# Gate projections between the attention's units, output by token tiles, one gate tile on another queue

## The chip, the cores and the metric

One core of one Trainium2 chip. The metric is device time in microseconds (us) of one execution. Three runs of the kernel before took 2414.84, 2416.75 and 2404.22 us; the median is 2414.84.

## The reference, cut to what matters

Two transformer layers run one after the other on x of 512 tokens by 1024 features, all in fp32. The first has a gated delta rule with four heads (`o_g`, chunks of 64 tokens, a state carried from chunk to chunk) and an attention with four heads (`o_n`: compressed, selected and windowed keys), then a gated feed-forward. The output of the delta rule is gated by a projection of the layer's input:

```python
o_g = rmsnorm(o_g, gdn_out_norm_w) * jax.nn.silu(gz.reshape(hd))
mixed = jnp.concatenate([o_g, o_n], axis=-1)
x = x + gate1 * (mixed @ w_out)
```

The second layer ends in a mixture of 16,384 experts: each token takes 16 of them for each of 8 heads, and the result is normalised.

```python
act = gelu(einsum('chkd,cd->chk', expert_u[experts], hc))
x = x + gate2 * einsum('chk,chkd->cd', gate * act, expert_v[experts])
return rmsnorm_2(x, final_g)
```

## The kernel before, in words

x is kept transposed: features on the 128 partitions in 8 blocks, 512 tokens along the row. A projection with 128 outputs is `gemm` (line 222): `weight` (line 200) loads 128x1024 fp32 through SP's queue, casts it on ScalarE (ACT) to a high part and subtracts on VectorE (DVE) for a low part (`split`, lines 196 to 198), and 8 blocks of three matmuls (high x high, high x low, low x high) fill one PSUM bank. The raw weight takes a buffer of the tag "raw" (three of them), the pair one of two.

The order of the instructions on each engine is not written by hand: a scheduler at build time takes them by the order of the code and by its own time model, and from then on each engine runs its queue in order. Buffers carry tags; a tile of a tag waits until one of that tag's buffers is free.

The first layer, from line 533: `nsa_begin`; for the pairs of heads (0, 1) and (2, 3) the projections q and v with `gdn_fin`, and `gdn_scan`, eight steps one after another that carry the state through small fp32 matmuls; then for the four tiles of 128 tokens, h = 0 to 3, the gate projection `proj_gz(h)` (line 661, its copy at line 662) and the attention `nsa(kp, h, h > 1)` (line 911). `nsa` has a compressed part (lines 921 to 941) and then four units, one per head (lines 942 to 968): two products of queries and keys, maximum, exponent into a tile "pr" of 128 x 2 x 512 (line 953), scaling, transposes through PSUM (line 963), copy to "pt", product with the values, copy of the result. "pr" has two buffers. Tiles 2 and 3 of the attention put the products into the two PSUM banks "acc", which the gate projections use too. At the end `gdn_out` (line 831) gates the scan's output, and the output projection follows.

The second layer's experts, `peer` (line 1127): a first stage forms the activations of all 128 groups of 128 experts, `spread` (line 1460) writes the gates of the tokens to DRAM in 22 blocks (a 23rd stays on the chip). The last stage, lines 1210 to 1280, goes through the 128 groups e: `gates` (line 1221) loads a gate tile for two groups (e = 0) or eight, from 22 blocks x 128 partitions, into "gtile" (two buffers); the activation is multiplied by its gate (line 1245), split, the group's 512 KB of weights are loaded and split, and `expert_out` adds into eight PSUM banks. Meanwhile `gather` (line 1323) fetches single experts' rows by indirect DMA on GpSimd's queue (POOL), and `gather_sum` (line 1336) adds them on DVE, 144 in all: 128 into `pN`, 16 into `pX`. After the last group the sums are folded into the banks (lines 1272 and 1273), x is updated, and `final` (line 1284) normalises: sums of squares over the features on TensorE, `r` by a power on GpSimd (line 1295), scaling by the gain (lines 1299 and 1301), transposes (line 1304), scaling by r (lines 1310 and 1312) and output (line 1313), one block of 128 features with all 512 tokens at a time.

Of the kernel before, what the change touches and what calls it, by code (L numbers as in the profile page):

```python
# [9 lines left out]
F32 = mybir.dt.float32  # L10
# [4 lines left out]
AF = mybir.ActivationFunctionType  # L15
ALU = mybir.AluOpType
# [4 lines left out]
P = 128  # L21
S = 512
D = 1024
KD = D // P
TT = S // P
# [129 lines left out]
class Builder:  # L155
# [304 lines left out]
    def block1(self):  # L460
        A, V, x = self.A, self.V, self.x
        with ExitStack() as st1:
            mp = self.mp = self.actp = self.pool(st1, "mp")
            gp = self.gp = self.pool(st1, "gd")
            self.ns = self.pool(st1, "ns")
            hst = ExitStack()
            hp = self.pool(hst, "h1", side="right")
            hi = hp.tile([P, KD, S], F32R, name="hi")
            lo = hp.tile([P, KD, S], F32R, name="lo")
            with ExitStack() as st2:  # L470
                self.ap = self.pool(st2, "ada", side="right")
                self.sqp = (self.ap, 3)
                for k in range(KD):
                    self.stat_add(k)
                self.dma(self.cols, A["cols"])
                self.sqp = (self.sm, 2)
                sw = self.cp.tile([P, KD], F32, name="swn1")
                ac = self.cp.tile([P, KD], F32, name="ac")
                self.C.activation(ac, self.col("c", 0, KD), AF.Silu)
                small = self.proj_small(hi, lo)  # L480
                started, weights = [], {}


                def mods(k):
                    v = self.mod(0, 1)[:, k:k + 1]
                    if k < 5:
                        self.dma(spare[k], A["ads"][k].rearrange("p k n -> p (k n)"))
                        ps = self.ps(5)
                        for i in range(KD):
                            self.mm(ps[:, 0:1], spare[k][:, i * P:(i + 1) * P], ac[:, i:i + 1], i == 0, i == KD - 1)  # L490
                        V.tensor_tensor(v, ps[:, 0:1], self.col("ada_b", KD + k), ALU.add)
                    else:
                        self.mod_tile(0, 1, k, buf=spare[k])
                    V.scalar_tensor_tensor(sw[:, k:k + 1], v, 1.0, self.col("n1", k), ALU.add, ALU.mult)
                    self.mod_tile(0, 0, k, 4)
                    if k in (0, 2, 5):
                        small.load()
                    if k in (3, 6):
                        started.append([self.next_bank(), 0, self.weight(A["w1"][len(started)].rearrange("p k n -> p (k n)"), D)])

                def steps(k, y):
                    small.step(k)
                    for s in started:
                        for i in range(s[1], k + 1):
                            self.mm3(s[0], s[2], i, hi, lo)
                        s[1] = k + 1
                spare = [v.rearrange("p h s -> p (h s)")[:, i * D:(i + 1) * D]
                         for v in (self.qA, self.vA, self.eq, self.kA) for i in range(2)]
                done = iter(range(KD))

                def upto(k):
                    for i in done:
                        mods(i)
                        if i == (3, 4, 4, 5, 5, 6, 7, 7)[k]:
                            break
                self.norm_mod(sw, self.mod(0, 0), hi, lo, lambda k: k in (0, 1, 3, 5, 6) and upto(k), steps, 3)
                small.end()
            with ExitStack() as st2:
                self.gi = self.pool(st2, "gi")
                self.pj = self.pool(st2, "pj")  # L520
                with ExitStack() as nst:
                    self.nk = self.pool(nst, "nk")
                    self.gdn_gates()
                    self.banks(2, 3)
                    for h in range(4):
                        self.proj_k(h, hi, lo, started[h][0] if h < len(started) else None)
                        self.gdn_inv(h)
                    self.banks()
                    self.proj_kv(hi, lo)
                    self.nsa_keys(self.nk)  # L530
                self.mod_queue(0, (2, 4, 3))
                self.proj_nq(hi, lo)
                kp = self.pool(st2, "nt")
                self.nsa_begin(kp)
                for pair in ((0, 1), (2, 3)):
                    for h in pair:
                        self.proj_qv(h, hi, lo)
                        self.gdn_fin(h)
                    self.gdn_scan(pair)
                for h in range(4):  # L540
                    self.proj_gz(h, hi, lo)
                    self.nsa(kp, h, h > 1)
            hst.close()
            self.ost = ExitStack()
            op = self.sqhp = self.pool(self.ost, "op", side="right")
            mh = self.mh = op.tile([P, KD, S], F32R, name="mh")
            ml = self.ml = op.tile([P, KD, S], F32R, name="ml")
            for h in range(4):
                self.split(mh[:, h, :], ml[:, h, :], self.nq[h])
            self.gdn_out()  # L550
            wx = self.pool(st1, "wx")
            self.more_weights(wx, 2)
            self.wring.reverse()
            self.banks(2, 3)
            first = self.gemms([A["wo"][m] for m in range(4)], mh, ml, 4)
            self.dma(x[:, 0:4, :], A["xt"][:, 0:4, :])
            self.dma(x[:, 4:8, :], A["xt"][:, 4:8, :])
            self.update(A["wo"], KD, mh, ml, self.mod(0, 2), beside=lambda: self.mod_run(2), first=first)
        self.more_weights()
        self.ffn()  # L560
# [97 lines left out]
            self.sumsq(self.nq[h], self.ssn[:, h, :])  # L658
            self.mod_run(4)

    def proj_gz(self, h, hi, lo):
        self.C.copy(self.gz[h], self.gemm(self.A["w1"][20 + h], KD, hi, lo))


    def gdn_gates(self):
# [242 lines left out]
        self.rq = rq.rearrange("p (h t) -> p h t", h=4)  # L908


    def nsa(self, kp, t, last):
        V, C, cb, kk, gs, kcn, vcn = self.V, self.C, self.cb, self.kk, self.gs, self.kcn, self.vcn
        neg = cb[:, 2 * P:3 * P]
        cm = cb[:, 9 * P:10 * P].rearrange("p (t n) -> p t n", t=TT)
# [27 lines left out]
        for h in range(4):  # L942
            pr = kp.tile([P, 2, S], F32, name="pr", bufs=2)
# [15 lines left out]
            for j in range(2):  # L959
# [6 lines left out]
                for kb in range(t + 1):  # L966
                    self.mm(oa, self.vn[:, kb, j, :], pt[:, kb * P:(kb + 1) * P], False, kb == t and j == 1)
            C.copy(self.nq[h][:, tb], oa)

    def ffn(self):  # L970
        A, V, C = self.A, self.V, self.C
# [155 lines left out]
    def peer(self):  # L1127
# [4 lines left out]
        with ExitStack() as st:  # L1132
# [77 lines left out]
            with ExitStack() as st2:  # L1210
# [10 lines left out]
                def gates(e):  # L1221
                    n = min(GA, P - e) if e else 2
                    if e:
                        gt = wk.tile([P, NB, GA, TB], F32, name="gtile", bufs=2)[:, :, :n, :]
                    else:
                        gt = self.hN[:, :NB * n * TB].rearrange("p (b a t) -> p b a t", b=NB, a=n)
                    self.dma(gt[:, :NB - 1], gd[:, :, e:e + n, :].rearrange("b p a t -> p b a t"))
                    C.copy(gt[:, NB - 1], gl[:, e:e + n, :])
                    return gt, e + n
                ahead_gt = gates(0)  # L1230
                for e in range(P):
# [20 lines left out]
                    vh, vl = vring[-1]()  # L1252
                    self.split(vh, vl, raw)
                    part.append((e, wh, wl, vh, vl))
                    self.gather_sum(2 if e % 6 == 0 else 1)
                    if e == P // 2:
                        self.dma(x, xs)
                    if e < P - LAST:
# [25 lines left out]
    def final(self, wk, sq, half):  # L1284
# [8 lines left out]
        V.tensor_scalar(ms, ss[:, 0:TT], 1.0 / D, EPS, ALU.mult, ALU.add)  # L1293
        r = wk.tile([P, TT], F32, name="fr")
        self.G.tensor_tensor(r, ms, self.mhalf[:, :TT], ALU.pow)
        xt = []
        for m in range(KD):
            if m % 2:
                C.activation(x[:, m, :], x[:, m, :], AF.Identity, scale=self.col("fin", m))
            else:  # L1300
                V.tensor_scalar(x[:, m, :], x[:, m, :], self.col("fin", m), None, ALU.mult)
            xt.append(self.ps(m) if m < 6 else self.acc())
            for t in range(TT):
                self.T.transpose(xt[m][:, t * P:(t + 1) * P], x[:, m, t * P:(t + 1) * P], self.ident)
        for m in range(KD):
            y = half().rearrange("p (t n) -> p t n", n=P)
            v = xt[m].rearrange("p (t n) -> p t n", n=P)
            if m in (1, 3, 5):
                for t in range(TT):
                    C.activation(y[:, t], v[:, t], AF.Identity, scale=r[:, t:t + 1])  # L1310
            else:
                V.tensor_tensor(y, v, r.unsqueeze(2).to_broadcast([P, TT, P]), ALU.mult)
            self.dma(self.out[:, :, m * P:(m + 1) * P], y)

    def expert_out(self, ps, m, part):
        mb = slice(m * P, (m + 1) * P)
# [204 lines left out]
```

## Time and profile before

| | |
|---|---|
| median of the runs | 2414.84 us |
| the profiled execution's own time | 2409.82 us |
| its span in the profile | 2407.7 us |
| TensorE matmul busy (PE) | 2333.4 us, 97% |
| weight load busy (PEld) | 2139.5 us, 89% |
| VectorE (DVE) busy | 1861.0 us, 77% |
| ScalarE (ACT) busy | 985.9 us, 41% |
| GpSimd (POOL) busy | 397.2 us, 16% |

Busy times of different engines overlap. PE's busy share is modelled, since matmuls are pipelined. The page cuts the span into 40 slices of 60.2 us; its line PEclk is the granted TensorE clock in tenths of full speed. Times in the rows are us from the span's start, and "idle before <- releaser" is how long the engine stood and what ended that.

### The profile page before, as it was taken

The page shows a single profiled execution, that of the slowest core. Times are in us where ns is not written, and L with a number is a line of the kernel's source. Part 1 is how long each engine was busy: PE and PEld are TensorE (multiplying, and loading weights), DVE is VectorE, ACT ScalarE, POOL GpSimd, SP SyncE. Part 2 cuts the span into 40 slices and gives each one's busy share as a digit, 9 for nine tenths or more (in the row PEclk, how much of TensorE's full clock was granted, in tenths as well). Part 3 has the DMA queues.
Part 4 walks back from the last instruction along what each step waited for, and adds up shares of the span by engine and source line. Part 5 has one row for each costly group of instructions (what it writes and reads, how often), then busy time and mean ns, then how long its engine had stood idle before and what let it go on. Part 6 is the DMA issues. An engine that isn't in the chain of part 4 may idle for free.

```text
span 2407.7 us, 35617 instructions
## 1 busy us (share of the span) xinstructions
PE 2333.4 (97%) x13159; PEld 2139.5 (89%) x13159; DVE 1861.0 (77%) x3833; ACT 985.9 (41%) x1623; POOL 397.2 (16%) x322
## 2 busy tenths in 40 slices
PE   7999999999999999999999999999998999999997
PEld 7788877878888888878899999989998999999997
DVE  6774546678886369774999999879995888888877
ACT  4633425344442233343333335446664333333333
POOL 0000000000000000000025342033320422323332
PEclk9999969999999999999999999999999999999998
DMA  7342101456666323242379997579997999999974
GB/s 275 126 139 71 62 10 53 145 180 195 196 193 192 102 80 97 71 151 81 115 258 319 346 351 283 170 256 359 354 331 256 369 363 349 352 346 347 351 255 150
DMA packets 205406, 523.67 MB, mean 217 GB/s; under 512 B 23728, under 2 KB 96048, under 8 KB 201648
## 3 DMA queue, kind: packets, MB, share of 16 engines
q1 hardware_dynamic: 163760, 370.38, 45.3%
q0 software_dynamic: 41472, 151.01, 17.6%
q8 instruction: 103, 1.69, 0.3%
q14 instruction: 71, 0.58, 0.1%
HBM read 475.21 MB, written 46.10 MB: 217 GB/s over the span
## 4 chain that ended last, share of the span: by engine, by line
PE 83%; DVE 8%; DMA 5%; ACT 2%; issue 1%; POOL 0%; SPq 0%; POOLq 0%; ACTq 0%; DVEq 0%
PE p L166 55%; PE acc L166 27%; DMA raw<-in_ada_dram 2%; DVE raw L401 1%; DMA gtile<-gdram 1%; DVE wlo L198 1%; DMA row<-in_eu_dram 1%; DVE o L1480 0%; DMA row<-in_er_dram,eidx 0%; ACT whi L197 0%; DVE rowlo L198 0%; ACT rowhi L197 0%; DVE grow L1333 0%; PE p L963 0%; DVE row L1333 0%
## 5 line engine op out<-in xcount | busy, mean ns | idle before, releaser
L197 ACT CAST rowhi<-row 128x1024 fp32r<-128x1024 f32 x226 | 236.8, 1050 | 410.7 <-issue 160.8
L198 DVE TENSOR_TENSOR rowlo<-row,rowhi 128x1024 fp32r<-128x1024 f32 x226 | 275.2, 1219 | 79.6 <-ACT rowhi L197 74.1
L197 ACT CAST whi<-raw 128x1024 fp32r<-128x1024 f32 (+2 forms) x152 | 150.5, 994 | 383.1 <-PE p L166 208.5
L1325 POOL DMA_INDIRECT grow<-in_ev_dram,eidx x135 | 176.4, 1307 | 399.5 <-DVE pN L1344 325.4
L198 DVE TENSOR_TENSOR wlo<-raw,whi 128x1024 fp32r<-128x1024 f32 (+2 forms) x152 | 174.6, 1151 | 86.9 <-ACT whi L197 85.4
L166 PE MATMUL p<-pwl,rowhi 128*128 128x368 f32 x576 | 193.2, 335 | 0.6 <-DVE pwl L198 0.6
L166 PE MATMUL p<-pwh,rowlo 128*128 128x368 f32 x576 | 189.1, 334 | 0.0
L166 PE MATMUL p<-lo,rowhi 128*128 128x368 f32 (+1 forms) x552 | 180.8, 329 | 0.9 <-DVE lo L368 0.9
L166 PE MATMUL p<-hi,rowhi 128*128 128x368 f32 (+1 forms) x552 | 178.9, 330 | 1.8 <-ACT hi L367 1.1
L166 PE MATMUL p<-hi,rowlo 128*128 128x368 f32 (+1 forms) x552 | 180.4, 330 | 0.0
L166 PE MATMUL acc<-hi,rowhi 128*128 128x368 f32 x512 | 171.7, 335 | 4.3 <-ACT rowhi L197 4.3
L166 PE MATMUL p<-hi,wlo 128*128 128x512 f32 (+1 forms) x464 | 172.2, 374 | 1.6 <-DVE wlo L198 1.6
L166 PE MATMUL p<-lo,whi 128*128 128x512 f32 (+1 forms) x464 | 172.3, 374 | 1.5 <-DVE lo L368 1.5
L166 PE MATMUL acc<-hi,rowlo 128*128 128x368 f32 x512 | 171.3, 335 | 2.4 <-DVE rowlo L198 2.4
L166 PE MATMUL p<-hi,whi 128*128 128x512 f32 (+1 forms) x464 | 168.3, 375 | 4.0 <-ACT hi L367 2.9
L166 PE MATMUL acc<-lo,rowhi 128*128 128x368 f32 x512 | 170.4, 333 | 0.0
L166 PE MATMUL p<-pwh,rowhi 128*128 128x368 f32 x576 | 153.6, 333 | 9.0 <-ACT pwh L197 7.5
L1325 POOL DMA_INDIRECT grow<-in_er_dram,eidx x91 | 115.7, 1271 | 235.5 <-DVE tv L1352 87.2
L1344 DVE SCALAR_TENSOR_TENSOR pN<-grow,dots,pN 128x1024 f32<-128x1024 f32 x119 | 152.2, 1279 | 0.7
L166 PE MATMUL acc<-hi,whi 128*128 128x512 f32 x352 | 141.5, 402 | 0.0
L166 PE MATMUL acc<-lo,whi 128*128 128x512 f32 x352 | 140.5, 399 | 0.0
L166 PE MATMUL acc<-hi,wlo 128*128 128x512 f32 x352 | 139.5, 397 | 0.0
(593 smaller groups left out, 6080.1 us busy)
## 6 DMA issues: line engine op xcount, KB each, us to landing
row<-in_eu_dram SPq DMA_DIRECT2D x128, 512.0 KB
row<-in_ev_dram SPq DMA_DIRECT2D x128, 512.0 KB
araw<-in_ada_dram SPq DMA_DIRECT2D x64, 512.0 KB
raw<-in_up_dram SPq DMA_DIRECT2D x44, 512.0 KB
gdram<-gstage SPq DMA_DIRECT2D x22, 1024.0 KB
gtile<-gdram SPq DMA_DIRECT2D x15, 1408.0 KB
spill<-pact SPq DMA_DIRECT2D x100, 184.0 KB
raw<-in_in_dram SPq DMA_DIRECT2D x28, 512.0 KB
```

The costliest lines, as they stand in the source:

```text
L166: self.T.matmul(out, lhsT, rhs, start=start, stop=stop)
L197: self.C.copy(hi, src)
L198: self.V.tensor_tensor(lo, src, hi.bitcast(F32), ALU.subtract)
L401: self.V.scalar_tensor_tensor(raw, raw, 1.0, self.act, ALU.mult, ALU.mult, accum_out=v)
L1325: self.G.indirect_dma_start(out=u, out_offset=None, in_=self.A[src], in_offset=bass.IndirectOffsetOnAxis(ap=self.eidx[:, s:s + 1], axis=0))
L1344: self.V.scalar_tensor_tensor(a, v, w, a, ALU.mult, ALU.add)
```

## The change

The gate projections move into the attention: all four are issued from within tiles 0 and 1, one behind the second and one behind the fourth unit of each, and their raw weight takes a buffer of the tag "pr". The gate tile that starts at e = 2 is loaded by a DMA of GpSimd's queue. Of the gathered sums, two instead of one are issued at the odd groups from 111 on. The output is formed by token tiles: two halves of 512 features, four tiles of 128 tokens each, each in one bank, scaled by one instruction and written as rows of 512 features.

```diff
                 for h in range(4):
-                    self.proj_gz(h, hi, lo)
-                    self.nsa(kp, h, h > 1)
+                    self.nsa(kp, h, h > 1, lambda i: h < 2 and i % 2 and self.proj_gz(2 * h + i // 2, hi, lo, kp))
...
-    def proj_gz(self, h, hi, lo):
-        self.C.copy(self.gz[h], self.gemm(self.A["w1"][20 + h], KD, hi, lo))
+    def proj_gz(self, h, hi, lo, kp):
+        stage = lambda: kp.tile([P, 2, S], F32, name="pr", bufs=2).rearrange("p a b -> p (a b)")
+        self.C.copy(self.gz[h], self.gemm(self.A["w1"][20 + h], KD, hi, lo, lane=(stage, None)))
...
-    def nsa(self, kp, t, last):
+    def nsa(self, kp, t, last, between):
...
             C.copy(self.nq[h][:, tb], oa)
+            between(h)
...
-                    self.dma(gt[:, :NB - 1], gd[:, :, e:e + n, :].rearrange("b p a t -> p b a t"))
+                    dma = self.G.dma_start if e == 2 else self.dma
+                    dma(gt[:, :NB - 1], gd[:, :, e:e + n, :].rearrange("b p a t -> p b a t"))
...
-                    self.gather_sum(2 if e % 6 == 0 else 1)
+                    self.gather_sum(2 if e % 6 == 0 or e >= KEPT and e % 2 else 1)
...
-        xt = []
-        for m in range(KD):
-            if m % 2:
-                C.activation(x[:, m, :], x[:, m, :], AF.Identity, scale=self.col("fin", m))
-            else:
-                V.tensor_scalar(x[:, m, :], x[:, m, :], self.col("fin", m), None, ALU.mult)
-            xt.append(self.ps(m) if m < 6 else self.acc())
+        H = KD // 2
+        for i in range(2):
+            bank = [self.ps(t) if i == 0 else self.ps(4 + t) if t < 2 else self.acc() for t in range(TT)]
+            for m in range(i * H, i * H + H):
+                if m < 5:
+                    C.activation(x[:, m, :], x[:, m, :], AF.Identity, scale=self.col("fin", m))
+                else:
+                    V.tensor_scalar(x[:, m, :], x[:, m, :], self.col("fin", m), None, ALU.mult)
+                for t in range(TT):
+                    self.T.transpose(bank[t][:, m % H * P:(m % H + 1) * P], x[:, m, t * P:(t + 1) * P], self.ident)
             for t in range(TT):
-                self.T.transpose(xt[m][:, t * P:(t + 1) * P], x[:, m, t * P:(t + 1) * P], self.ident)
-        for m in range(KD):
-            y = half().rearrange("p (t n) -> p t n", n=P)
-            v = xt[m].rearrange("p (t n) -> p t n", n=P)
-            if m in (1, 3, 5):
-                for t in range(TT):
-                    C.activation(y[:, t], v[:, t], AF.Identity, scale=r[:, t:t + 1])
-            else:
-                V.tensor_tensor(y, v, r.unsqueeze(2).to_broadcast([P, TT, P]), ALU.mult)
-            self.dma(self.out[:, :, m * P:(m + 1) * P], y)
+                y = half()
+                if t % 2:
+                    C.activation(y, bank[t], AF.Identity, scale=r[:, t:t + 1])
+                else:
+                    V.tensor_scalar(y, bank[t], r[:, t:t + 1], None, ALU.mult)
+                self.dma(self.out[:, t, i * S:(i + 1) * S], y)
```

`KEPT` is 111, `S` 512, `P` 128, `TT` 4, `KD` 8. The PSUM banks have the tags p0 to p5, one bank each (`ps`), and "acc", two banks.

## Rows read from the trace of the kernel before

**Rows 1.** The page's 40 slices: granted clock in tenths, GB/s of the DMA engines.
```profile
PEclk9999969999999999999999999999999999999998
...
GB/s 275 126 139 71 62 10 53 145 180 195 196 193 192 102 80 97 71 151 81 115 258 319 346 351 283 170 256 359 354 331 256 369 363 349 352 346 347 351 255 150
```
**Rows 2.** Stretches around the attention: length, busy us (instructions) by engine, granted clock, DMA.
```profile
275.00:298.00 23.00, 23.00 (x123) 19.07 (x123) 9.12 (x18) 5.35 (x9) 0.00 (x0) 1.00 0.20 69
298.00:306.00 8.00, 7.06 (x35) 4.87 (x34) 4.30 (x12) 3.81 (x7) 0.00 (x0) 0.92 0.21 67
306.00:352.00 46.00, 44.21 (x156) 35.95 (x155) 16.91 (x67) 12.73 (x45) 0.00 (x0) 0.50 0.00 1
352.00:430.00 78.00, 74.85 (x472) 59.99 (x470) 49.37 (x150) 37.08 (x90) 2.90 (x1) 1.00 0.16 50
```
**Rows 3.** Groups of lines, 275 to 298 us: busy us, mean ns, idle before.
```profile
L166 PE MATMUL acc<-hi,wlo 128*128 128x512 f32 x22 | 9.0, 409 | 0.0
...
L197 ACT CAST whi<-raw 128x1024 fp32r<-128x1024 f32 x3 | 3.1, 1046 | 13.6 <-PE acc L166 13.6
L198 DVE TENSOR_TENSOR wlo<-raw,whi 128x1024 fp32r<-128x1024 f32 x2 | 2.4, 1218 | 1.9 <-ACT whi L197 1.9
```
**Rows 4.** Instructions of line 662: ns shortest, median, longest; first and last start.
```profile
L662 ACT COPY x<-acc x4: 578/579/582, 282.5 to 393.5; 128x512 f32<-128x512 f32 x4
```
**Rows 5.** Timelines of PE and ACT: second transposes of a unit, exponent of another.
```profile
307.36 0.42 PE L963 MATMUL p<-ca,pr 128*128 128x128 f32 x1
...
327.76 0.42 PE L963 MATMUL p<-ca,pr 128*128 128x128 f32 x1
...
307.98 0.46 ACT L953 ACTIVATE pr<-p,mx,rq 128x128 f32<-128x128 f32 x1
...
328.43 0.57 ACT L953 ACTIVATE pr<-p,mx,rq 128x256 f32<-128x256 f32 x1
```
**Rows 6.** Chain that ended last, at the attention's end: a 512 KB load.
```profile
418.53 4.35 DMA raw<-in_ada_dram
```
**Rows 7.** Line 817, a scan step's subtraction: all of them, and two on DVE's timeline.
```profile
L817 DVE TENSOR_TENSOR w<-kA,p x16: 405/419/427, 258.5 to 402.0; 64x256 f32<-64x256 f32 x16
...
350.40 0.42 DVE L817 TENSOR_TENSOR w<-kA,p 64x256 f32<-64x256 f32 x1 [2.62 <-PE p L166]
...
357.68 0.41 DVE L817 TENSOR_TENSOR w<-kA,p 64x256 f32<-64x256 f32 x1
```
**Rows 8.** Two stretches ahead of the attention, columns as in rows 2.
```profile
208.00:212.00 4.00, 4.00 (x15) 3.58 (x15) 0.16 (x1) 0.59 (x1) 0.00 (x0) 0.50 0.56 221
212.00:216.00 4.00, 4.00 (x29) 3.61 (x27) 0.00 (x0) 0.00 (x0) 0.00 (x0) 0.93 0.02 4
```
**Rows 9.** Chain that ended last, before the expert loop.
```profile
1847.66 16.16 DMA gtile<-gdram
```
**Rows 10.** Timeline of PE, first matmuls on the second gate tile.
```profile
1864.97 2.21 PE L166 MATMUL p<-pwh,rowhi 128*128 128x368 f32 x6 [5.54 <-ACT pwh L197]
```
**Rows 11.** DMA queues from 1847 to 1864 us: packets, MB, share of 16 engines.
```profile
q1 hardware_dynamic: 3943, 2.42, 50.7%
q0 software_dynamic: 864, 3.15, 47.6%
```
**Rows 12.** Gathers of the expert loop, line 1325, columns as in rows 4.
```profile
L1325 POOL DMA_INDIRECT grow<-in_ev_dram,eidx x135: 937/998/3039, 1848.4 to 2372.3; - x135
```
**Rows 13.** Timelines of DVE and PE: the last two sums, and their fold.
```profile
2376.75 2.60 DVE L1344 SCALAR_TENSOR_TENSOR pX<-grow,dots,pX 128x1024 f32<-128x1024 f32 x2 [0.25 <-DMA grow<-in_ev_dram,eidx]
...
2382.14 0.29 PE L166 MATMUL p<-fold,pX 128*128 128x16 f32 x2
```
**Rows 14.** The output: timelines of ACT and SP, and a stretch of it.
```profile
2396.66 3.21 ACT L1310 ACTIVATE grow<-p,fr 128x128 f32<-128x128 f32 x12 [5.33 <-POOL fr L1295]
...
2397.38 6.35 SPq L1313 DMA_DIRECT2D out_dram<-grow  x8
...
2400.00:2404.00 4.00, 0.00 (x0) 0.00 (x0) 0.00 (x0) 0.00 (x0) 0.00 (x0) 0.50 0.98 288
```

## The prediction

> **What bounds the kernel now.** I read the page's slices first [rows 1]: TensorE is busy nearly everywhere, and its granted clock stands at 0.9 and above in every slice but the sixth, 301 to 361 us, and the last; the sixth lies in the first block's attention. Cut into stretches [rows 2], this gives: to 298 us a clock of 1.00, from 306 to 352 us 0.50 with PE shown busy for 44.21 of 46 us, from 352 us full again. 0.50 is the lower of its two levels, 1.2 GHz. So in these 46 us TensorE is not waiting; it does its small fp32 matmuls at half speed, and up to 46 x 0.5 = 23 us are there to be won.
>
> What stands where is read from the groups of lines in 275 to 298 us [rows 3] and from the gate copies [rows 4]. 66 of the 96 matmuls of the four gate projections (8 blocks x 3 matmuls each) run in those 23 us, where PE is full anyway; the first copy is at 282.5 us, the last at 393.5. The half-clock stretch that follows has none. The fourth projection comes late, since its bank has the tag "acc" that units of tiles 2 and 3 also take.
>
> The attention itself is paced by its two buffers "pr": the exponent of unit k+2 starts right behind the second transposes of unit k, at 307.36 and 307.98, and again at 327.76 and 328.43 [rows 5]; so it goes for eight units in a row, to the second of tile 2, and from the one exponent to the other it is three units, 6.8 us each. Tiles of one tag are handed out in the order of the code here (that is how I read rows 4 and 5), so a gate weight that asks for "pr" behind unit 1 cannot be loaded before a slot of units 0 and 1 is free: this really moves the projections.
>
> **Gate projections between the units.** Removed from 275 to 298 us: 66 matmuls. PE holds 123 matmuls there in 23 us [rows 2]: if all cost the same, the 66 take 23 x 66/123 = 12.3 us of them, by their columns (512 against 128 for the others) 23 x 33,792/41,088 = 18.9. I take 15. So what stands behind them comes up to 15 us earlier; I take 13, since the steps ahead of unit 0 have a latency of their own. Then unit 0's slot is free at about 307.4 - 13 = 294 us. The load takes 4.35 us from issue to landing (a weight of the same 512 KB [rows 6]), the cast 1.05, the remainder 1.22 [rows 3]: the first projection starts at about 300 us. The clock, which fell about 8 us after the last dense matmuls, at 306 [rows 2], would fall at about 281. Dense matmuls brought it back within 4 to 8 us at 208 to 216 us [rows 8]; so it stays low from 281 to about 304, 23 us in place of 46. **Gain: (46 - 23) x 0.5 = 11.5 us**, if it stays up through the other three projections, which follow every two units, some 13 us at half clock and less at full.
>
> What this displaces: the four weights take a turn of 4.35 + 1.05 + 1.22 = 6.6 us each in the ring. With two slots half of that, 13 us in all, shows where the ring sets the pace; the 13 us of the earlier start pay for it, so I take 0, with ends of +13 and -13. The scan has room: its 16 steps span 258.5 to 402.0 us, while two neighbouring steps, nearly all at half clock, are 7.3 us apart [rows 7], so 15 intervals could do with 109 of 143 us. On SP the four loads now wait for a slot, and the loads of the output projection stand behind them; nobody reads these before the attention ends. On ACT the casts waited 13.6 us for TensorE in 275 to 298 us [rows 3]; they will wait for a landing instead, with exponents behind them, the same kind of stall. I round to **-11 us**, from 0 to -23.
>
> **Gate tile of expert 2 through GpSimd.** In the chain the tile is issued at 1847.66, right behind the last matmul on the buffers whose room it takes, and lands 16.16 us later [rows 9]; TensorE stands 5.54 us for it [rows 10]. It is 22 x 128 = 2,816 runs of 512 bytes. From the queues in that stretch [rows 11] a packet costs 0.507 x 17 us x 16 / 3,943 = 35 ns on SP's queue and 0.476 x 17 x 16 / 864 = 150 ns on GpSimd's: the tile alone would need 2,816 x 35 / 16 = 6.2 us, the six gathers beside it 6 x 128 x 150 / 16 = 7.2. 6.2 + 7.2 and some 2.8 of latency are the 16.2 seen. On GpSimd's queue the tile stands ahead of the six gathers, so it no longer shares with them; but SP now sends the next tile, as large, at the same moment: 6.2 + 6.2 + 2.8 = 15.2. I take **0**. Ends: with all engines to itself it lands 6 us sooner; and if GpSimd needs per row what a gather shows, 0.94 us for 128 rows at the shortest [rows 12], its 2,816 rows take 20.7 us, the tile lands at about 1848.4 + 20.7 + 2 = 1871 and the gathers behind it as late: +7. SP loses one issue, and no one waits for SP there; queued behind the tile on GpSimd are the gathers, and behind those the sums on DVE. A gain here would run into the sums: their last one ends at 2379.35, only 2.8 us before TensorE folds them in [rows 13].
>
> The trace shows all engines taken: the two queues together hold 98% of them [rows 11]. The Trainium skill, "DMA: Bandwidth & Descriptors", section "Issuing engines are not separate DMA queues", says that transfers from SP, ACT and GpSimd share the same 16 engines and that another issuer saves only issue time; by it this edit gives nothing, and by the first-byte figures of the same page of the Trainium skill (about 1 us from GpSimd, 0.6 from SP) it costs an estimated 0.4 us. The trace agrees as to the sharing; no run here shows the first byte.
>
> **Sums earlier.** 135 of the 144 gathered rows go into the expert loop's buffers [rows 12], so 9 sums stand ahead of it; with one per expert and two at every sixth the 144 end at expert 114 today, and at expert 113 with the extra ones at 111 and 113. Two sums move by one to three experts. DVE and GpSimd cover them, and their end has the 2.8 us of room above: 0; without that cover a sum costs its 1.3 us on DVE [rows 13].
>
> **Output by token tiles.** The 32 transposes, 8 scalings, 8 outputs and 8 DMAs stay. Removed: the 12 short activations, 0.27 us each, 3.2 us in a row today [rows 14]; four outputs of 128x512 on ACT, and four on DVE, take their place, at an estimated 0.65 us, half of what a sum over 1,024 columns takes [rows 13], 2.6 us in a row: -0.6 (ends: half and twice that, -1.9 and +2.0). Each DMA now writes runs of 2 KB, not 512 bytes. Today eight issues take 6.35 us from 2397.38 and the engines move 288 GB/s at a share of 0.98 [rows 14]. At the 369 GB/s of the best slice [rows 1] I estimate 2.1 MB in 5.7 instead of 7.3 us: -1.6. Together **-2 us**, from 0 to -4. The scalings go from four on each of ACT and DVE to five and three; squares on ACT could slip by one scaling, which the range holds.
>
> **Sum.** -11 + 0 + 0 - 2 = -13 us against the profiled execution's 2409.82: 2396.8. That execution is 5.0 us under the median of the runs, 2414.84; taken over to the median: **2402 us**. A measurement of this kernel can tell some 0.5% from no change, 12 us here: below 2402.8 and above 2426.9.
>
> **Rivals.**
> 1. The clock holds through all four projections and the gap ahead of them as well: -23 - 2, **2390 us**. For it: from 352 us attention and scan alone keep the clock at 1.00 [rows 2]. Against: a slot is free only after tile 0's compressed part.
> 2. The low stretch only moves: it starts 25 us earlier and lasts as long, since four scattered blocks of 24 matmuls are not dense enough. The change then doesn't do what it says: -2, **2413 us**. For it: the rise at 352 came without any large matmuls, so I don't know what decides.
> 3. The ring becomes the bound, slower than before. Each weight holds one of two slots for 6.6 us with nothing computed from it; if TensorE meanwhile has no other work, all four turns show: 26 less the 13 of the earlier start, and -2 at the end, 2414.84 + 11 = **2426 us**. It decides if the second unit behind each weight is late by the whole turn. For it: every exponent in the pattern of rows 5 waits on a slot already. Against: the scan fills TensorE.
> 4. GpSimd writes the tile's descriptors as slowly as its gathers: +7 for the tile and some +2 on DVE for late gathers, -13 + 9: **2411 us**.
>
> **How the numbers follow.** Forecast 0.37, rival 1 0.17, rival 2 0.16, rival 3 0.13, rival 4 0.17. Faster by over 0.5%: 0.23 of the forecast's 0.37, since its value lies just under that bound, all 0.17 of rival 1, and 0.07 from rivals 2 and 4 with the better ends of the other terms: 0.47. Slower by over 0.5%: half of rival 3, which lies at the bound, and 0.04 where it and rival 4 meet: 0.11. Within 0.5%: 0.42. The range takes rival 1 with the better ends of the small terms at one side, 2384, and stops at 2422 on the other, inside rival 3.
>
> **What would show it.** Right: no gate copy before 300 us, one about every 10 us after; a low clock for 20 to 25 us instead of 46; the attention's stretch, to 430 us in rows 2, over by about 419; the tile for expert 2 landing within 3 us of 16; the last stretch behind the experts shorter by 2 us. Wrong: a clock that is low for 40 us or not at all, a wait of over 10 us for the tile, or exponents that come 13 us late behind each weight.

## The result and the profile after

Slower: median 2424.09 us over 20 runs, against 2412.09 us for the kernel before, also over 20; ratio 1.0064, 95% interval 1.0048 to 1.0079. I had predicted 2402, and nothing above 2422. The profiled execution after has a span of 2428.6 us, 20.9 more than before: 10.0 of these are there when the output projection starts, 13.1 come between that and the fold of the sums, and the output gives 2.2 back (the rows for each follow).

**The attention.** Stretches of the kernel after, columns as in [rows 2]:

```profile
280.00:300.00 20.00, 17.62 (x92) 14.30 (x92) 9.37 (x25) 5.31 (x11) 0.00 (x0) 0.76 0.00 1
300.00:320.00 20.00, 19.75 (x92) 15.89 (x90) 7.62 (x27) 5.99 (x20) 0.00 (x0) 0.81 0.16 53
320.00:340.00 20.00, 18.44 (x76) 15.24 (x76) 9.66 (x35) 6.74 (x18) 0.00 (x0) 0.74 0.00 1
340.00:360.00 20.00, 20.00 (x109) 16.76 (x110) 7.60 (x23) 7.28 (x21) 0.00 (x0) 0.91 0.11 32
360.00:380.00 20.00, 17.97 (x104) 14.39 (x102) 10.38 (x27) 11.70 (x20) 0.00 (x0) 0.98 0.23 75
380.00:400.00 20.00, 19.85 (x98) 14.87 (x99) 12.65 (x42) 9.25 (x28) 0.00 (x0) 0.85 0.00 0
400.00:420.00 20.00, 17.00 (x103) 13.66 (x102) 13.57 (x41) 7.98 (x18) 2.90 (x1) 0.83 0.33 104
420.00:440.00 20.00, 19.48 (x121) 17.05 (x119) 11.96 (x28) 7.97 (x20) 0.00 (x0) 0.83 0.32 107
```

No stretch is at half clock throughout, as 306 to 352 us was [rows 2], but none keeps full clock either. Half-clock time is 2 x (1 - granted clock) x length: 51 us between 280 and 440, against 48 before, now in five dips; 17 of the 51 lie ahead of 320 us, 34 behind. Added up, PE's columns show 150.1 us busy of 160, that is 9.9 idle; before has 6.5. The same stretch before, in one line:

```profile
280.00:440.00 160.00, 153.49 (x792) 123.24 (x791) 81.46 (x247) 62.57 (x155) 2.90 (x1) 0.85 0.15 47
```

The gate copies, and three stretches of 4 us, show where the clock returns:

```profile
L663 ACT COPY x<-acc x4: 579/587/588, 313.6 to 373.8; 128x512 f32<-128x512 f32 x4
...
304.00:308.00 4.00, 4.00 (x15) 3.40 (x16) 2.16 (x6) 1.26 (x6) 0.00 (x0) 0.56 0.00 0
308.00:312.00 4.00, 4.00 (x20) 3.02 (x18) 0.15 (x1) 0.27 (x1) 0.00 (x0) 1.00 0.01 2
...
320.00:324.00 4.00, 2.95 (x10) 2.36 (x10) 1.85 (x4) 2.32 (x6) 0.00 (x0) 0.65 0.01 4
```

The first gate block, which ends at 313.6, does bring the clock back, at 308; by 324 it has fallen again, in a stretch where PE stands 1.05 of 4 us. Pauses of PE at four of the five dips, and the first matmul of the output projection (timeline of PE; what ended the idle time stands in brackets):

```profile
288.95 0.43 PE L166 MATMUL p<-qA,w 128*128 128x64 f32 x2 [0.51 <-DVE w L824]
...
321.10 0.76 PE L166 MATMUL acc<-hi,whi 128*128 128x512 f32 x1 [1.05 <-ACT whi L197]
...
380.15 1.65 PE L166 MATMUL acc<-kw,x 128*128 128x384 f32 x2 [1.37 <-ACT pr L954]
...
415.10 1.04 PE L940 MATMUL p<-ca,sc 128*32 128x128 f32 x4 [2.02 <-DVE sc L937]
...
440.65 0.73 PE L166 MATMUL p<-mh,whi 128*128 128x512 f32 x2 [0.88 <-ACT mh L197]
```

Only one of the four pauses waits for a gate weight (whi, at 321.10); the others are the scan's and the attention's own steps. The output projection starts at 440.65 us, where before it was 430.64.

**The gate tile.** The chain of waits after, at the place of [rows 9]:

```profile
1859.42 21.16 DMA gtile<-gdram
1880.58 0.02 issue
1880.61 0.49 DVE x L1248
1881.10 0.31 DVE pact L1248
1881.40 0.11 issue
1881.51 0.54 DVE vact L1248
1882.05 1.35 DVE pact L1248 x3
1883.40 0.45 DVE vact L1248
1883.86 1.14 DVE rowlo L198
1884.99 2.26 DVE x L1248 x5
...
1889.75 0.46 DVE pwl L198
1890.21 0.04 issue
1890.25 4.05 PE p L166 x12
```

The tile that is waited for was issued by SP at 1859.42: it is expert 10's. GpSimd issued expert 2's at 1859.59 and spent 1.42 us on it. The first x, the pact and the vact are the activations of experts 10 to 16: DVE multiplies these seven first and comes to expert 2 (the second x) only at 1884.99. From the issue to TensorE's first matmul on a pwl that needs the tile, 1859.42 to 1890.25, it is 30.8 us; before, 1847.66 to 1868.05, it was 20.4. TensorE's pause ahead of its first matmuls on the tile, 5.54 us before [rows 10], has tripled (timeline of PE):

```profile
1886.04 2.21 PE L166 MATMUL p<-pwh,rowhi 128*128 128x368 f32 x6 [16.81 <-ACT pwh L197]
```

**The output.** Timelines of PE, ACT and SP after, and a stretch, as in [rows 13, 14]:

```profile
2405.21 0.29 PE L166 MATMUL p<-fold,pX 128*128 128x16 f32 x2
...
2419.76 1.84 ACT L1312 ACTIVATE grow<-p,fr 128x512 f32<-128x512 f32 x3 [5.80 <-POOL fr L1298]
...
2420.48 4.46 SPq L1315 DMA_DIRECT2D out_dram<-grow  x8
...
2422.00:2426.00 4.00, 0.00 (x0) 0.00 (x0) 0.49 (x1) 0.19 (x1) 0.00 (x0) 0.50 1.02 383
```

From the fold to the span's end it is 23.4 us, before 25.6; the engines move 383 GB/s, before 288.

### The profile page after: what moved, and what is told of

Same layout as the page of the kernel before. It is cut to its first block, busy times and chain, and to the rows that moved or that the text cites. A ratio compares the mean times of both kernels' runs of the same rounds, so it can differ in the third digit from the quotient of the medians.

```text
span 2428.6 us, 35611 instructions
## 1 busy us (share of the span) xinstructions
PE 2334.9 (96%) x13159; PEld 2139.9 (88%) x13159; DVE 1861.6 (77%) x3831; ACT 989.3 (41%) x1616; POOL 412.7 (17%) x323
## 4 chain that ended last, share of the span: by engine, by line
PE 80%; DVE 11%; DMA 5%; ACT 2%; issue 2%; POOL 0%; SPq 0%; POOLq 0%; DVEq 0%; ACTq 0%
PE p L166 53%; PE acc L166 26%; DMA raw<-in_ada_dram 1%; DVE o L1482 1%; DVE row L1335 1%; DMA row<-in_er_dram,eidx 1%; DMA gtile<-gdram 1%; DVE rowlo L198 1%; DVE wlo L198 1%; DVE raw L401 1%; DMA araw<-in_ada_dram 0%; ACT whi L197 0%; PE p L964 0%; DVE o L1471 0%; DVE wqrlo L198 0%
## 5 line engine op out<-in xcount | busy, mean ns | idle before, releaser
L1327 POOL DMA_INDIRECT grow<-in_ev_dram,eidx x135 | 170.6, 1264 | 361.3 <-DVE pN L1346 325.7
L1327 POOL DMA_INDIRECT grow<-in_er_dram,eidx x91 | 127.1, 1396 | 222.4 <-DVE tv L1354 85.5
```

Of the source, the lines that this page charges most:

```text
L1327: self.G.indirect_dma_start(out=u, out_offset=None, in_=self.A[src], in_offset=bass.IndirectOffsetOnAxis(ap=self.eidx[:, s:s + 1], axis=0))
```

## The experiments

Each kernel was timed beside the kernel before. Ratios carry a 95% interval; one of ±0.0025 is ±6 us.

### The parts alone

e1_proj: the kernel before with only the first four pieces of the diff (gate projections between the units, weights in pr).

> The kernel before with the gate projections between the units alone. In the profile of the changed kernel the first output-projection matmul comes 10.0 us later than before (440.65 for 430.64). Of that, 6 us arise ahead of the attention, at 206 to 225 us, where the order of TensorE's matmuls is the same in both and only the granted clock came back later; I take that for a matter of the single execution. Theory A (the clock falls again between the projections): 2 to 6 us slower than before; half-clock time between 280 and 445 us 40 to 55 us, in four or more dips, and the scan's steps (line 818 there) no farther apart at full clock than before. Rival B (the two slots of pr are the bound): 2 to 6 us slower too, but TensorE idle between 280 and 440 us is over 14 us against some 6 before, and the half-clock time under 35 us. Rival C (it gains as predicted, and all 10 us are chance): 5 to 11 us faster, first output-projection matmul before 425.

Ratio 1.0017 (0.9993 to 1.0042), some 4 us slower if anything. Between 280 and 440 us:

```profile
280.00:440.00 160.00, 150.43 (x775) 122.47 (x776) 82.84 (x246) 65.04 (x156) 2.90 (x1) 0.84 0.14 47
```

That is 51 us of half clock and 9.6 idle. It fits theory A; B wanted over 14 us of idle time, C a gain.

e2_tile: only `dma = self.G.dma_start if e == 2 else self.dma`.

> The kernel before with the gate tile of expert 2 on GpSimd's queue alone. Theory A (the order on DVE: the scheduler's model takes the GpSimd transfer for the later one, so DVE multiplies six activations by the tile of expert 10 before the first by the tile of expert 2): 8 to 12 us slower; from the issue of the tile to TensorE's first matmul on it some 30 us, where before has 20.4; DVE's first multiply behind the wait is on the tile of expert 10. Rival B (GpSimd's transfer itself is slow): as much slower, but the first multiply on the tile of expert 2 has a wait of its own of over 2 us that ends in a DMA. Rival C (no price, as predicted): within 3 us of before.

Ratio 1.0034 (1.0009 to 1.0059), 8 us slower. DVE's timeline:

```profile
1860.49 0.54 DVE L1246 TENSOR_TENSOR x<-x,gtile 128x368 f32<-128x368 f32 x1 [16.89 <-DMA gtile<-gdram]
...
1864.80 3.71 DVE L1246 TENSOR_TENSOR x<-x,gtile 128x368 f32<-128x368 f32 x8
```

The eight multiplies for experts 2 to 9 come behind, with no wait of their own: their tile was there already. A, not B.

e3_out: only the new `final`.

> The kernel before with the output by token tiles alone. Theory (fewer, longer scalings and longer runs in the transfer): 1.5 to 2.5 us faster; from the fold's matmul to the end 23.4 us where before has 25.6. Rival (the 2 us are given back ahead of the fold, or the scheduler orders something else in another way): within 1 us of before.

Ratio 0.9986 (0.9960 to 1.0013). The interval can't show 2 us; the profile does: the fold's matmul is at 2380.27, the end at 2404.0, so 23.7 us where before has 25.6.

The sums were not timed alone. The program built with only that edit has on all five engines the instructions of the kernel before in the same order; only the buffers of some gathers change.

### The order on DVE

e5_both: `if e in (2, 10)`, both tiles through GpSimd.

> The kernel before with both gate tiles, of experts 2 and 10, on GpSimd's queue; DVE's order is then the one of before, expert 2's eight multiplies first. Theory A (order): the price of the tile edit is gone: within 3 us of before, or faster by up to 5, since the first tile has the engines to itself; from the issue of the first tile to TensorE's first matmul on it 14 to 21 us. Rival B (GpSimd's transfers are slow in themselves): at least as slow as with one tile, 8 us or more, and DVE's first wait is over 18 us.

Ratio 0.9982 (0.9956 to 1.0008); 14.7 us below e2_tile by the medians (2402.25 and 2416.91). DVE, with both its order and its first wait changed (GpSimd issued the tile at 1856.38):

```profile
1869.32 3.71 DVE L1246 TENSOR_TENSOR x<-x,gtile 128x368 f32<-128x368 f32 x8 [8.84 <-DMA gtile<-gdram]
```

This also takes expert 10's tile off SP. e8_dep leaves it there and changes DVE's order; for that a small copy moves from ACT to DVE:

```diff
-                    C.copy(gt[:, NB - 1], gl[:, e:e + n, :])
+                    e != GA + 2 and C.copy(gt[:, NB - 1], gl[:, e:e + n, :])
...
+                    if e == GA + 1:
+                        z = wk.tile([P, 1], F32, name="z", bufs=1)
+                        V.tensor_scalar(z, act[:, :1], 0.0, None, ALU.mult)
+                        V.tensor_scalar(ahead_gt[0][:, NB - 1], gl[:, e + 1:e + 1 + GA, :], z, None, ALU.add)
```

> The kernel before with the gate tile of expert 2 on GpSimd's queue and that of expert 10 on SP's, as in the change, but the last block of the second tile is copied on DVE behind the multiply for expert 9, so that DVE's multiplies stand in the order of the experts. Theory A (the price of the tile edit is DVE's order): the 8 us are gone: 4 us faster to 2 us slower than before; TensorE idle under 6 us where it waits for expert 2; DVE waits 9 to 15 us for the tile. Rival B (the two transfers at once slow each other, order or not): 4 us slower or more, DVE waits over 17 us.

Ratio 0.9990 (0.9964 to 1.0016). The chain of waits, and DVE's timeline:

```profile
1844.89 11.65 DMA gtile<-gdram
```

```profile
1856.57 3.70 DVE L1246 TENSOR_TENSOR x<-x,gtile 128x368 f32<-128x368 f32 x8 [3.90 <-DMA gtile<-gdram]
```

On GpSimd's queue, with the other tile on SP's at the same time, expert 2's tile lands in 11.65 us, not 16.16. So the tile landed 4.5 us sooner, and the order made a loss of it. That is shown: e2_tile and e8_dep have the same two issues and differ, up to the first matmuls on the tile, in DVE's order. TensorE's pause ahead of these, 5.54 us before [rows 10], is 16.77 us in e2_tile, 4.43 in e5_both and 3.15 in e8_dep. DVE's own wait is only 3.90 us, where I had expected 9 to 15; it has another subtraction to do in between.

e9_after_both: the changed kernel with `if e in (2, 10)`.

> The changed kernel with the gate tile of expert 10 on GpSimd's queue too, which puts DVE's order right. Theory A: of the 12 us that the change costs, 8 to 13 go with it; 1 us faster to 4 us slower than before. Rival B (something else of the change costs most of it): still 7 us slower or more.

Ratio 1.0005 (0.9987 to 1.0024). A: nearly all of the loss goes when DVE's order is put right. As in e5_both, expert 10's tile has left SP too. Against e10_best further down, which differs from it in the place of the gate projections and the sums alone, it is 0.26% slower, some 6 us, with an interval wider than that.

### The place of the gate projections

e6_raw puts them at the same places, with weights in "raw" and tied to the unit:

```diff
+                    self.nsa(kp, h, h > 1, lambda i: h < 2 and i % 2 and self.proj_gz(2 * h + i // 2, hi, lo, self.nq[i][:, h * P:h * P + 1]))
...
         self.dma(r, dram)
+        if getattr(self, "tie", None) is not None:
+            self.V.scalar_tensor_tensor(r[:, :1], self.tie, 0.0, r[:, :1], ALU.mult, ALU.add)
```

> The kernel before with the gate projections at the places that the change gives them, but with weights that pass through the three buffers raw, loaded ahead; a small addition on DVE, of zero times the unit's result, keeps each behind its unit. No weight takes a slot of pr. The kernel with the projections in pr (the first experiment) had TensorE idle for 9.6 us and at half clock for 51 us between 280 and 440 us. Theory A (the turns in pr make TensorE pause, and behind every pause the clock falls): idle there under 7 us, half clock under 40 us, time 5 us faster to 1 us slower than before, mean granted clock above the 0.980 of the first experiment. Rival B (four scattered dense blocks let the clock fall wherever their weights come from): idle under 7 us as well, but half clock at 45 us or more in four or more dips, 2 to 5 us slower than before. Rival C (the ring costs nothing): idle still over 9 us.

Ratio 1.0029 (1.0010 to 1.0047):

```profile
280.00:440.00 160.00, 151.73 (x758) 121.47 (x757) 78.45 (x243) 61.90 (x150) 2.95 (x1) 0.81 0.14 47
```

61 us at half clock, 8.3 idle. The mean granted clock of its runs is 0.978, below e1_proj's 0.980 and the 0.981 of before. Theory A falls: without a turn in pr the clock is no better. B is nearest, though the idle time stays over its 7 us. The output projection starts at 439.91, no earlier than with the turns (435.52 in e1_proj, 440.65 after). The edit brings a tie of its own, on DVE, so what the turns cost by themselves is not measured.

e11_last (`for h in range(4): self.proj_gz(h, hi, lo)` behind the attention's loop) and e12_first (the same loop inside, at `if h == 2`, ahead of `self.nsa`):

> The kernel before with all four gate projections behind the attention in the code; their copies then stand behind the last units on ACT, so no dense block lies among the units of tiles 0 to 2 and none ahead of them. The last experiment with scattered blocks and weights loaded ahead had 61 us at half clock and 8.3 us of TensorE idle between 280 and 440 us. Theory D (it is the missing dense work ahead of the first units that costs: without it TensorE runs into the attention's and the scan's own waits earlier, and the clock falls earlier): idle over 7.5 us up to the output projection, the first fall of the clock at 295 us or before, 2 us or more slower than before. Theory E (the scattered blocks themselves make the clock fall again): with none scattered, half clock of 48 us or less and time within 2 us of before.

> The kernel before with all four gate projections called ahead of tile 2 in the code; by the order on ACT all four then run ahead of the attention's units (three of them do in the kernel before). Theory D (dense work ahead of the units is where it costs least): idle between 280 and 440 us of 6 us or less, half clock anywhere from 13 to 48 us as in the kernels with that stretch unchanged, time within 3 us of before at equal granted clock. Theory E: the same or faster. Rival (the fourth projection is needed as filler among the later units): idle 8 us or more, 3 us or more slower.

Ratios 0.9954 (0.9933 to 0.9975) and 0.9954 (0.9927 to 0.9980): both 11 us faster than before. For e11_last neither theory had that; for e12_first E had it ("the same or faster"). Gate copies and the stretch, first of e11_last, then of e12_first:

```profile
L663 ACT COPY x<-acc x4: 573/577/578, 404.4 to 424.3; 128x512 f32<-128x512 f32 x4
...
280.00:440.00 160.00, 153.60 (x842) 124.46 (x841) 83.56 (x252) 62.60 (x156) 2.90 (x1) 0.91 0.13 40
```

```profile
L664 ACT COPY x<-acc x4: 575/579/582, 285.9 to 309.1; 128x512 f32<-128x512 f32 x4
...
280.00:440.00 160.00, 153.69 (x822) 123.69 (x822) 82.35 (x250) 63.34 (x156) 2.90 (x1) 0.89 0.14 47
```

Idle 6.4 and 6.3 us, half clock 29 and 35. D's slowdown without dense work ahead is refuted. The output projection starts only 2 to 5 us earlier than before (425.42 and 428.27); the rest comes later. Between 480 and 520 us, at the start of the feed-forward, PE is idle for 1.8 us at a clock of 0.96 in e11_last, against 5.1 and 0.87 before: the scheduler's order there is another. ACT shows it, at the second group of normalised blocks; before, then e11_last, then e6_raw:

```profile
492.35 1.71 ACT L367 ACTIVATE hi<-ny,mod 128x256 fp32r<-128x256 f32 x4 [5.55 <-DVE ny L366]
```

```profile
484.64 1.77 ACT L367 ACTIVATE hi<-ny,mod 128x256 fp32r<-128x256 f32 x4 [2.02 <-DVE ny L366]
```

```profile
497.93 1.76 ACT L369 ACTIVATE hi<-ny,mod 128x256 fp32r<-128x256 f32 x4 [1.69 <-DVE ny L368]
```

From ACT's first `hi<-ny,mod` to its first `gh<-fa` the 11 profiles with the order of before or of e1_proj take 38.1 to 40.1 us, the five with the new one (e6_raw, e11_last, e12_first and two kernels below) 32.6 to 34.9. So some 5 of the 11 us come with this order. It doesn't need the projections in one piece: e6_raw has them among the units and the same 5 us are already in its ratio of 1.0029.

### Together

e10_best: e5_both and the new `final`. e13_dep_out: e8_dep and the new `final`. e14_again: the changed kernel once more.

> The kernel before with the two parts that gained alone: both gate tiles on GpSimd's queue, and the output by token tiles; the gate projections stay where they were. Theory: the gains add, 4 to 9 us faster than before. Rival (they are the chance of the granted clock): within 2 us of before, at equal clock too.

> The kernel before with the gate tile of expert 2 on GpSimd's queue, that of expert 10 on SP's, DVE's order put right by the copy that depends on expert 9, and the output by token tiles. Theory: at equal granted clock 3 to 6 us faster than before (the first alone gave 3 to 4, the output 1.5); by the medians 4 to 10. Rival: no better than both tiles on GpSimd's queue with the output, 2 to 3 us at equal clock.

> The changed kernel once more, beside the kernel before on the same chip as these runs. If the parts add (gate projections 3 to 4 us slower, tile 8, output 2 to 3 faster), it is 8 to 10 us slower; the first measurement gave 12. If the parts make each other worse, 12 or more.

0.9979 (0.9955 to 1.0004), 0.9956 (0.9926 to 0.9986) and 1.0068 (1.0045 to 1.0092). The first gains about what was expected, though its interval reaches no change; the second gains more surely. The changed kernel is 16 us slower by the ratio, past the 12 at which I had expected to say that its parts make each other worse, while the parts (0.17 + 0.34 - 0.14%) give 9; the parts' intervals of ±6 us each cover the gap, so that stays open.

e15_last_dep_out and e16_first_dep_out: e13_dep_out with e11_last's and e12_first's place.

> The kernel before with three parts: all four gate projections behind the attention, the gate tile of expert 2 on GpSimd's queue with DVE's order put right, and the output by token tiles. If the gain of the projections lies in their place (0.46% alone), it adds to the 0.44% of the other two: 16 to 24 us faster than before. If it came from another order that the scheduler chose downstream, in the feed-forward or the experts, it need not come back: 6 to 14 us faster.

> The same with all four gate projections ahead of the attention's units. If their place is what gains (0.46% alone): 16 to 24 us faster than before. If it was the scheduler's order downstream: 6 to 14 us faster; if the two kernels differ by over 8 us, the place matters, and then dense work behind the units or ahead of them is not the same.

0.9917 (0.9885 to 0.9949), median 2391.19, and 0.9936 (0.9910 to 0.9963), median 2393.76: 20 and 15 us faster than before. These two beat both kernels. The first lies where the place was to gain, the second between the two theories; the intervals of both overlap that of e13_dep_out, so they fit a gain that adds and no more. They don't tell the theories apart either: up to the expert loop, at about 1800 us, every engine has the order of e11_last in the one and of e12_first in the other, so the order downstream was the same again. That the gain lies in the place is not shown.

### One kernel, seven executions

In six of these kernels (e2_tile, e3_out, e5_both, e8_dep, e10_best, e13_dep_out) every engine has the same instructions in the same order as before until far behind the attention. So their profiles and that of before are seven executions of one attention:

| | half clock 280 to 440, us | PE idle, us | output projection starts |
|---|---|---|---|
| before | 48 | 6.5 | 430.64 |
| e2_tile | 13 | 5.9 | 415.31 |
| e3_out | 22 | 5.9 | 426.81 |
| e5_both | 48 | 5.9 | 435.75 |
| e8_dep | 35 | 5.9 | 422.97 |
| e10_best | 42 | 5.9 | 426.84 |
| e13_dep_out | 42 | 6.8 | 427.87 |
| gates among units: after, e1_proj, e9_after_both, e14_again | 51, 51, 45, 61 | 9.9, 9.6, 10.2, 9.4 | 440.65, 435.52, 437.29, 442.47 |

The lines for the best and the worst of the unchanged attention, e2_tile and then e5_both:

```profile
280.00:440.00 160.00, 154.06 (x856) 123.86 (x855) 89.82 (x259) 67.13 (x162) 2.90 (x1) 0.96 0.18 57
...
415.31 0.74 PE L166 MATMUL p<-mh,whi 128*128 128x512 f32 x2 [0.87 <-ACT mh L197]
```

```profile
280.00:440.00 160.00, 154.12 (x804) 124.06 (x803) 84.82 (x255) 63.13 (x156) 2.90 (x1) 0.85 0.13 43
...
435.75 0.73 PE L166 MATMUL p<-mh,whi 128*128 128x512 f32 x2 [0.87 <-ACT mh L197]
```

Same code, and the output projection starts 20 us apart; some 8 of the 20 come from low clock ahead of the attention (granted clock 0.94 and 0.66 between 200 and 230 us). Half-clock time is 36 us on the mean of the seven, 13 to 48; with the gates among the units it is 52 on the mean of four, 45 to 61. In these four the second, third and fourth dip last 10, 3 and 7 us each time, at the same steps; only the first and the last vary. With the projections in one piece the output projection starts at 418 to 428 us (e11_last, e12_first, e15_last_dep_out, e16_first_dep_out), inside the 415 to 436 of the unchanged attention: a gain in the attention itself isn't shown.

## Why the prediction was wrong, point by point

**What bounds the kernel now: wrong, and the root of the error.** "Up to 46 x 0.5 = 23 us are there to be won" took the half-clock stretch of one execution for a property of the kernel. The seven executions above put it anywhere from 13 to 48 us, and mine was at the upper end. The three runs of before that I had were 12 us apart; I read that as noise around a fixed stretch, where much of it is low-clock time that comes and goes. Over all runs timed in the experiments, a straight line of time on mean granted clock, with a level of its own for each kernel, gives 2.0 us per 0.001 of clock and leaves a scatter of 2.6 us; the runs of before alone go from 2388.96 us at 0.991 to 2422.68 at 0.975.

**Gate projections between the units, -11: wrong, about +4 measured.** Right were the small steps: no copy before 300 us, the first gate matmul at 305.1 (I had 300), the clock back within some 4 us of it, and a first dip of 17 us (I had 23). The clock fell first at about 290 us, not 281; that it falls 8 us behind the last dense matmuls was one execution too: in the seven it fell first between 302 and 324 us. The step that failed is "Gain: (46 - 23) x 0.5 = 11.5 us, if it stays up through the other three projections". It did not stay up: the four dips behind the first add 34 us, which I had at none. Behind each gate block TensorE went back to the small matmuls of scan and attention and the clock fell again, in or right behind a 4 us stretch in which PE stood for 0.5 to 2 us. Rival 2 (the low stretch only moves) was nearest, rival 1 (the clock holds throughout) has nothing for it. The copies came 20 us apart, where I had 10. That each pause causes its fall is argued from their places; it was not tried.

"What this displaces ... I take 0" held as to the ring: rival 3's 13 us lie outside the interval of e1_proj (-2 to +10 us), and e6_raw, which has no turns, is no faster. But 3.4 us more of idle time came with the place, which no term had. One reading of mine was wrong without harm: the two scan steps of [rows 7] are not "nearly all at half clock", since full clock returns at 352 us [rows 2]; steps within the half-clock stretch are 4.8 to 11.3 us apart. The scan had room all the same, 139 us after for its 16 steps.

**Gate tile, 0 with ends of -6 and +7: wrong, +8 measured, and by a mechanism not in the text.** I had worked out the transfer (15.2 us; 11.65 measured in e8_dep, near the lower end) and looked for what is queued behind it on GpSimd. What I left out is DVE: its order is fixed at build time, and with the tile on GpSimd's queue the seven multiplies of the next tile were put first, whenever either lands. That the scheduler's time model took GpSimd's transfer for the later one is my reading of that order; it was not looked at. "The tile for expert 2 landing within 3 us of 16" was the wrong thing to look for; the landing that counted was expert 10's, 21.16 us. "A wait of over 10 us for the tile" was the right one: 16.81. Rival 4's descriptors are refuted: 1.42 us on POOL.

**Sums, 0: right** as far as the order goes; no run times them. **Output, -2: right**, 1.9 to 2.2 us from the fold to the end in e3_out and after, with 383 GB/s where I estimated 369. Over all profiles that stretch is 22.3 to 24.7 us with the new output (eight) and 24.6 to 25.7 with the old (eight), 1.5 apart on the mean.

**The numbers.** The sum had -13 us; 12 slower was measured. Two terms of -11 and 0 came out at some +4 and +8, each with ±6. The chance of slower, 0.11, hung on the ring alone; a wrong order on an engine downstream of the moved transfer was no rival at all.

## What to carry to other kernels

A stretch at the lower clock in one profile can be a draw: before it enters a sum, look at several executions, or at the spread of the runs beside their granted clock. Where a scheduler fixes the order at build time, moving a transfer to another queue can also move its users in every other engine's queue; compare those orders, and tie the second user to the first with a small true dependence if they swap. Do the same before a gain is put down to a place: the kernels with the dense matmuls in one piece were 11 us faster, some 5 of these by another order in the feed-forward. Dense matmuls forced between small ones cost here, some 4 to 7 us by three ratios (e1_proj, e6_raw, and e9_after_both against e10_best).

## What the runs showed of the hardware

The granted clock differs for the same instructions. Ahead of the attention 16 matmuls stand between the same neighbours in both kernels (timeline of PE, before and then after):

```profile
213.24 1.86 PE L166 MATMUL p<-blk,cw 128*128 128x32 f32 x16
```

```profile
213.65 3.46 PE L166 MATMUL p<-blk,cw 128*128 128x32 f32 x16
```

The clock fell at the same place, during 32 such matmuls at 202 to 206 us, and came back at about 212 us in one execution and 225 in the other; this alone is 6 us of the 10 by which the attention's end was late in the profile after.

Where two queues kept the same engines busy, they took turns by packets, not by bytes. The kernel after from 1870 to 1878 us (packets, MB, share of 16 engines):

```profile
q0 software_dynamic: 738, 2.68, 88.1%
q1 hardware_dynamic: 737, 0.38, 16.6%
```

One packet each, 3.6 KB on GpSimd's queue against 0.5 KB on SP's, so in this stretch SP's tile, in runs of 512 bytes, got a seventh of the bytes that GpSimd's queue got: expert 10's landed after 21.16 us. One to one is not the rule of every stretch; in [rows 11], with gathers still being issued, it was 864 to 3,943. On GpSimd's queue, ahead of the gathers, expert 2's tile took 11.65 us in e8_dep. The Trainium skill, "DMA: Bandwidth & Descriptors", section "Issuing engines are not separate DMA queues", says that another issuer saves only issue time, as the engines are shared. The runs agree that they are shared (88.1 and 16.6%), but here the tile landed 4.5 us sooner from another issuer (11.65 against 16.16), more than the issues themselves cost (0.4 us on SP, 1.4 on GpSimd). That this is so because the issuer set what the tile had to take turns with is argued, not isolated.
